# The weight sums for the seven-product down projection: from VectorE in the mix to GpSimd in the mix and VectorE in the up projection; the sample's squares split in one piece

## The chip, the cores and the metric

One NeuronCore of one Trainium2 chip runs the whole step in one launch. The metric is the time of an execution on the device, in microseconds. Engines are named as the profile names them: PE (matmul), PEld (its weight loads), DVE (VectorE), ACT (ScalarE), POOL (GpSimd), SP (SyncE, which here only issues transfers).

## The reference, cut to what matters

One layer of a decoder is computed for 512 prompt tokens and 64 sample tokens (8 sequences of 8). Two attention branches come first. What the change touches comes behind them:

```python
br_fox = o_fox @ w_br_fox;  br_nsa = o_nsa @ w_br_nsa          # 512 -> 1024 each
mix = sigmoid(mg[:, :1024]) * br_fox + sigmoid(mg[:, 1024:]) * br_nsa   # mg = h @ w_in[:, last 2048]
x = x + gt1 * (mix @ w_out)
h = rms_norm(x, norm2_g) * (1 + sc2) + sh2
u = relu(h @ w_up)                                             # 1024 -> 4096
y = x + gt2 * ((u * u) @ w_down)                               # 4096 -> 1024
```

All of it is in float32, and all weights are read from HBM once per launch.

## The kernel before, in words

**Precision.** PE multiplies in a rounded format. Every float32 operand is therefore split into a high part (a copy by ACT into the rounded format) and a low part (operand minus high part, on DVE): `split`, lines 113 and 132 in the profile. A product is made of three matmuls, high by high, low by high, high by low. A weight is loaded into a raw tile by SP, split, and only then multiplied. The raw tiles of most weights come from one ring of three, with the tag "raw".

**Seven products.** The up projection (from its fourth pair of weight columns on) and most of the down projection use Strassen's scheme in the form with seven products instead of eight. It needs sums and differences of weight quarters. For down, with rows 0 to 1535 of `w_down` as upper half, rows 1536 to 3071 as lower half, and columns halved, they are b12 - b11, then b22 minus that, b22 - b11 and b21 - b22. The kernel makes them ahead of time: `down_sums(pool, k)` (line 1956) handles one of twelve row blocks of 128. It loads two tiles of 128 x 1024 ("td", SP, line 1961), makes four differences of 128 x 512 in place (DVE, line 101, the helper `tt`), and stores both tiles to HBM tiles `tD` (POOL, line 1966). The "td" tiles come from a ring of three. The products T1 to T4 of down read `tD` back ("wdrT").

**The mix** (`mix_part`, line 1878). For each of eight column blocks e and each branch x: a gate product "mg" (48 matmuls), tanh on ACT into "mgt", a branch product "br" (24 matmuls), and on DVE (line 110) mgt = (mgt + 1) * br, which frees the PSUM banks of br. PE has four banks for these, so it can be two products ahead. Behind both branches the two mgt are added (POOL for e below 7, line 1950) and the sum is split into `mix2`. In e = 1 to 6 two calls of `down_sums` follow. Weights are raw tiles "wmr" and "wbr", split into "wmh"/"wml" and "wbh"/"wbl".

**Out and up** (`out_part`, `mlp_up`, line 2177). The output projection's weights "wo" are split into rooms that lie where the mix's tiles were; wo3 lies over the td tiles. In `mlp_up` each pair n of weight columns goes through seven products "up<n>a", "up<n>b" and "up<n>e", 12 matmuls each, in an order written out by hand. The sums of the up weights (`pair_weights`, line 2158; "sums<-pu") are POOL's from pair 5 on. DVE splits the weights ("wp") and reads PSUM between the products that accumulate into one bank ("u<-up6b" and so on). `squares_out` relus, squares and stores u to HBM: `sD` (blocks for the seven-product part) or `uD`.

**Down** (`mlp_down`, line 2241). Seven products p = 0 to 6 over three chunks c of 512 rows each; PE's groups "dn" are the prompt's, "dns" the sample's (p = 0, 1, 4, 5). For dns, `sample_part` (line 2111) loads one block of squares ("sr", POOL), and splits it into a room "sa": one load, one ACT copy, one subtraction per chunk. The first block is made ahead, in up (`u_load`, line 2119). The tile that "sr" is loaded to, with the tag "us", lies over the last u tile of up (u15) in the built program, so it waits for u15's store.

**What sets the order.** Each engine runs its instructions in the order that the tile scheduler gives them when the program is built. An instruction that waits holds everything behind it on its engine. `issue_after` and `pinned` only push an instruction behind another one in that order; they add no wait on the chip. The helper `dma` keeps the transfers of one queue in the order in which they are written. A tile from a ring waits until the tile that had its place is read for the last time, a stored one until its store has landed.

Of the kernel before, what the change touches and what calls it, by code (L numbers as in the profile page):

```python
# [6 lines left out]
F32 = mybir.dt.float32  # L7
# [7 lines left out]
P = 128  # L15
# [31 lines left out]
class Step:  # L47
# [1830 lines left out]
    def mix_part(self, pq, pr, mix2):  # L1878
# [55 lines left out]
        for e in range(NK):  # L1934
            if e == 0:
                ws = [weights(0, x) for x in range(2)]
                for k in range(8):
                    self.split(oH[:, k], oL[:, k], self.oT[:, k])
                m = [gate(e, x, ws[x][0], True) for x in range(2)]
                for x in range(2):  # L1940
                    branch(e, x, ws[x][1], m[x])
            else:
                m = []
                for x in range(2):
                    mg, br = weights(e, x)
                    m.append(gate(e, x, mg))
                    branch(e, x, br, m[x])
            if e == NK - 1:
                self.wo0 = self.out_weights(0)
            (nc.gpsimd if e < NK - 1 else nc.vector).tensor_tensor(m[0], m[0], m[1], op=OP.add)  # L1950
            self.split_pack(mix2[:, e], m[0])
            if 0 < e < NK - 1:
                for k in range(2 * e - 2, 2 * e):
                    self.down_sums(pq, k)

    def down_sums(self, pool, k):

        b = [pool.tile([P, D], F32, tag="td", bufs=3, name=f"td{k}_{i}") for i in range(2)]
        for i in range(2):
            r0 = SQ * 512 * i + P * k  # L1960
            self.nc.sync.dma_start(b[i], self.I["w_down"][0, r0:r0 + P, :])
        (b11, b12), (b21, b22) = [[t[:, 512 * h:512 * h + 512] for h in range(2)] for t in b]
        for out, x, y in ((b11, b12, b11), (b12, b22, b12), (b22, b22, b11), (b21, b22, b21)):
            self.tt(out, x, y, OP.subtract)
        for i in range(2):
            self.nc.gpsimd.dma_start(self.tD[k // 2][:, k % 2, i], b[i])
# [144 lines left out]
    def sample_part(self, pool, tag, blk, room):  # L2111

        x = pool.tile([P, 4, NS], F32, tag=tag, bufs=3, name=f"sr{blk}_{self.turn}")
        self.turn += 2
        self.dma("gpsimd", x, self.sD[blk][:, 2048:2304].rearrange("p (k t) -> p k t", k=4))
        self.split(room[:, :, 0:NS], room[:, :, NS:P], x)
        return room

    def u_load(self, q):
# [6 lines left out]
        elif q == 2:  # L2126
            self.first_sample = self.sample_part(self.praw, "raw", 0, self.both[:, 4096:4608].rearrange("p (k t) -> p k t", k=4))
# [49 lines left out]
    def mlp_up(self, pu, h3):  # L2177
# [27 lines left out]
        for n in range(FIRST, NP + 1):  # L2205
# [15 lines left out]
            if 0 <= n - NP + 6 < 4:  # L2221
                self.u_load(n - NP + 6)
# [18 lines left out]
    def mlp_down(self, pf):  # L2241
# [26 lines left out]
        left = [self.ph.tile([P, 2, 4, 256], F32, tag="h3", bufs=2, name=f"s2{i}") for i in range(2)]  # L2268
        left = [left[c // 2][:, c % 2] for c in range(SQ)]
# [26 lines left out]
        for p, key in enumerate(("11", "21", "T3", "T2", "T1", "22", "T4")):  # L2296
            pbs = [self.mmb(f"dn{p}{m}") for m in range(2)]
            sample = {0: 0, 1: 1, 4: 0, 5: 1}.get(p)
            if sample is not None and p != 5:
                sb = self.accb(f"dns{p}")  # L2300
            for c in range(SQ):
# [12 lines left out]
                if sample is not None:  # L2314
                    x = self.first_sample if p + c == 0 else self.sample_part(
                        pf, "us", c + SQ * sample, pf.tile([P, 4, P], F32R, tag="sa", bufs=3, name=f"sa{p}_{c}"))
                    for k in range(4):
                        for e in range(2):
                            self.mm(sb, x[:, k], w[e][:, k], c + k + e == 0 and p != 5, c == SQ - 1 and k + e == 4 and p != 4)
# [30 lines left out]
        for blk in range(2 * SQ, NBLK):  # L2350
# [8 lines left out]
            if not last:  # L2359
                x2 = [self.pb.tile([P, 4, D], F32, tag="x", bufs=1, name="x2b")]  # L2360
                x2 = [x2[0][:, i] for i in range(4)] + [pf.tile([P, D], F32, tag="x2s", bufs=1, name="x2s")]
                for i, (t0, m) in enumerate(TILES):
                    self.dma("sync", x2[i][:m], self.x2D[:m, i])
                with self.tc.issue_after(self.last_mm):
                    gp = self.gate_prompt(self.ph, 40, 1.0, "2", tag="h3", bufs=2)
                    gx = pf.tile([P, NT], F32, tag="u", bufs=3, name="gx2")[:, 0:512]
                    gs = self.gate_sample(self.ph, 40, 1.0, "2", gx.rearrange("p (k b t) -> p k b t", k=NK, t=8), tag="h3", bufs=2)
# [218 lines left out]
```

## Time and profile before

| what | us |
|---|---|
| median of 3 runs (1206.57 to 1213.69) | 1207.56 |
| the profiled execution's own time | 1211.11 |
| its span, first to last instruction | 1209.4 |
| PE busy | 1144.4 |
| DVE busy | 814.3 |
| ACT busy | 582.0 |
| POOL busy | 203.1 |

The stages in the profiled execution, by PE's groups: attention to about 587, the mix from there to 759, out to 817, up to 1008 (with down's first chunk pulled in at 999), down to the end. In lists of groups a row gives line, engine, operation, tiles (out<-in), shapes and count, then busy time and mean duration of one, then the idle time of the engine just before these instructions and what ended it. In timelines a row gives start and duration, then the engine; a bracket gives the idle time before it and the releaser. In tables by stretch there are, for each engine, busy time and instructions; then PE's granted clock (1.00 is full), the busy share of the transfer engines and GB/s.

### The profile page before, as it was taken

How to read it: one execution, taken by the hardware profiler on the slowest of the kernel's cores; microseconds unless marked ns; L12 is line 12 of the kernel's file. 1: busy time of each engine (PE TensorE's matmuls, PEld its weight loads, DVE VectorE, ACT ScalarE, POOL GpSimd, SP SyncE). 2: the span in 40 equal slices, each digit the busy share in tenths (PEclk: the TensorE clock that was granted, in tenths of full speed). 3: DMA queues.
4: the chain of work that ended last, by engine and by line, in shares of the span. 5: the costliest groups of instructions: out<-in, count | busy, mean ns of one | idle time of the engine just before them, and what ended most of it. 6: DMA issues, size and time to landing. Idle time of an engine off the chain costs nothing.

```text
span 1209.4 us, 24525 instructions
## 1 busy us (share of the span) xinstructions
PE 1144.4 (95%) x9051; PEld 979.7 (81%) x9051; DVE 814.3 (67%) x2000; ACT 582.0 (48%) x1183; POOL 203.1 (17%) x254
## 2 busy tenths in 40 slices
PE   4999999999999999999879899999999996999998
PEld 4887789999666656776779789889999995888887
DVE  3787785686788856665555463677877753788686
ACT  2554453454777755545412222447555654564520
POOL 3303000001211130000312120001556401101100
PEclk9999999999999899999989999999999998999999
DMA  9897556794776359989989983437454538857742
GB/s 219 212 250 229 156 152 220 249 329 160 254 236 209 99 164 311 299 284 293 308 260 270 264 262 110 130 93 223 150 161 151 187 102 252 308 183 264 234 133 79
DMA packets 188091, 255.48 MB, mean 211 GB/s; under 512 B 23065, under 2 KB 145634, under 8 KB 185794
## 3 DMA queue, kind: packets, MB, share of 16 engines
q1 hardware_dynamic: 150402, 185.61, 50.5%
q0 software_dynamic: 17456, 53.74, 13.6%
q10 hardware_dynamic: 20112, 14.55, 4.2%
q8 instruction: 71, 1.16, 0.4%
q14 instruction: 50, 0.41, 0.1%
HBM read 217.64 MB, written 57.12 MB: 227 GB/s over the span
## 4 chain that ended last, share of the span: by engine, by line
PE 72%; DMA 13%; DVE 6%; issue 4%; ACT 3%; SPq 1%; POOL 1%; ACTq 0%; DVEq 0%; POOLq 0%
PE dn L78 13%; PE z L78 6%; PE hid L78 6%; PE wo L78 4%; DMA td<-in_w_down 3%; PE up L78 3%; PE mg L78 3%; PE ss L78 2%; PE ct L84 2%; DMA tD<-td 2%; PE dns L78 2%; PE k L84 2%; PE br L78 2%; PE so L78 1%; PE ada L78 1%
## 5 line engine op out<-in xcount | busy, mean ns | idle before, releaser
L78 PE MATMUL z<-winh,h 128*128 128x264 f32 (+1 forms) x576 | 111.0, 286 | 0.3
L78 PEld LDWEIGHTS z<-winh,h 128*128 128x128 f32 x576 | 91.7, 190 | 2.1 <-DVE h L800 0.9
L78 PE MATMUL z<-winl,h 128*128 128x264 f32 (+1 forms) x320 | 88.2, 284 | 0.1
L78 PE MATMUL mg<-hH,wmh 128*128 128x288 f32 x256 | 77.0, 302 | 9.9 <-DVE mgt L110 9.5
L78 PE MATMUL mg<-hH,wml 128*128 128x288 f32 x256 | 76.4, 300 | 0.9 <-DVE wml L132 0.9
L113 ACT ACTIVATE xh<-ct 128x256 fp32r<-128x256 f32 x128 | 48.0, 384 | 56.4 <-PE ct L84 29.5
L78 PE MATMUL mg<-hL,wmh 128*128 128x288 f32 x256 | 74.1, 300 | 0.3 <-DMA hL<-hfd 0.3
L132 DVE TENSOR_TENSOR xl<-ct,xh 128x256 fp32r<-128x256 f32 x128 | 51.7, 420 | 14.5 <-ACT xh L113 12.7
L78 PEld LDWEIGHTS z<-winl,h 128*128 128x128 f32 x320 | 60.6, 190 | 0.3 <-DVE winl L132 0.3
L78 PEld LDWEIGHTS mg<-hH,wmh 128*128 128x128 f32 x256 | 49.4, 193 | 10.6 <-DVE mgt L110 9.8
L78 PEld LDWEIGHTS mg<-hH,wml 128*128 128x128 f32 x256 | 49.3, 193 | 1.1 <-DVE wml L132 1.1
L78 PEld LDWEIGHTS mg<-hL,wmh 128*128 128x128 f32 x256 | 48.2, 192 | 0.8 <-DMA hL<-hfd 0.7
L101 DVE TENSOR_TENSOR td<-td,td 128x512 f32<-128x512 f32 x24 | 16.6, 690 | 47.0 <-DMA td<-in_w_down 46.8
L78 PE MATMUL br<-oH,wbh 128*128 128x288 f32 x128 | 38.7, 302 | 8.1 <-DVE mgt L110 8.1
L78 PE MATMUL hid<-xh,w1hlk 128*128 128x512 f32 (+1 forms) x160 | 45.2, 370 | 1.2 <-ACT xh L113 1.2
L132 DVE TENSOR_TENSOR wp<-sums,wp 128x1024 fp32r<-128x1024 f32 x26 | 39.3, 1520 | 8.8 <-ACT wp L113 8.3
L78 PE MATMUL hid<-xh,w1hlv 128*128 128x512 f32 (+1 forms) x160 | 44.0, 362 | 0.4 <-ACT xh L113 0.4
L132 DVE TENSOR_TENSOR wp<-pu,wp 128x512 fp32r<-128x512 f32 (+1 forms) x26 | 31.2, 1206 | 16.5 <-ACT wp L113 16.0
L84 PE MATMUL ct<-identF,ro 128*128 128x128 f32 x256 | 36.4, 282 | 6.1 <-DVE ro L116 5.1
L113 ACT ACTIVATE wbh<-wbr 128x512 fp32r<-128x512 f32 x16 | 10.0, 631 | 61.0 <-DMA wbr<-in_w_br_nsa 38.1
L113 ACT ACTIVATE u<-u 128x1152 f32<-128x1152 f32 x29 | 33.7, 1161 | 10.2 <-DVE u L101 9.7
L78 PE MATMUL br<-oL,wbh 128*128 128x288 f32 x128 | 38.0, 297 | 0.0
(1180 smaller groups left out, 3670.8 us busy)
## 6 DMA issues: line engine op xcount, KB each, us to landing
adw<-in_w_ada SPq DMA_DIRECT2D x16, 1024.0 KB
foxD<-in_cache_fox_kv SPq DMA_DIRECT2D x128, 128.0 KB
fr<-foxD SPq DMA_DIRECT2D x28, 512.0 KB
sr<-in_cache_nsa_kv SPq DMA_DIRECT2D x112, 128.0 KB
cpg<-in_cache_nsa_kv SPq DMA_DIRECT2D x104, 128.0 KB
pu<-in_w_up SPq DMA_DIRECT2D x26, 512.0 KB
wdr<-in_w_down SPq DMA_DIRECT2D x26, 512.0 KB
td<-in_w_down SPq DMA_DIRECT2D x24, 512.0 KB
```

What stands on the lines that cost most here:

```text
L78: ins = self.nc.tensor.matmul(out, a, b, start=start, stop=stop, skip_group_check=True)
L84: ins = self.nc.tensor.transpose(out, in_, self.identF[:n, :n])
L101: self.nc.vector.tensor_tensor(out, a, b, op=op)
L113: return self.nc.scalar.activation(out, in_, f, **kw)
L132: self.splits.append((eng or self.nc.vector).tensor_tensor(l, x, h.bitcast(F32), op=OP.subtract).ins)
```

## The change

- In the mix, `down_sums` runs for eight of the twelve row blocks, in e = 1 to 6 (one block or two each). The loads, the four differences and the stores are all POOL's now, in its own queue. The two mgt are added by DVE in all e.
- The other four row blocks are made in up, two at a time: loaded by SP in n = 5 and 8 (two transfers of 1 MB each), the four differences (now 128 x 2 x 512) on DVE in n = 6 and 9, stored by POOL in n = 7 and 10. Their tile is the room "x" of the pool `pb`, which held R before and holds the first split token blocks ("as") behind.
- `u_load` comes one n later.
- In down, `sample_part` makes all blocks of one product in one piece: for p = 0 blocks 1 and 2 (128 x 8 x 64), for p = 1, 4, 5 three blocks (128 x 12 x 64). Loads stay one per block. The room "sa" is in the pool `ph` ("h3"); the raw tile "us" is a single one, and in the built program it lies over T0, an operand of up that PE reads for the last time in pair 15's first product E. The three tiles of differences "s2" and the late gates move to a tag "late" of the pool `pf`.

```diff
-            (nc.gpsimd if e < NK - 1 else nc.vector).tensor_tensor(m[0], m[0], m[1], op=OP.add)
+            nc.vector.tensor_tensor(m[0], m[0], m[1], op=OP.add)
             self.split_pack(mix2[:, e], m[0])
-            if 0 < e < NK - 1:
-                for k in range(2 * e - 2, 2 * e):
-                    self.down_sums(pq, k)
+            for k in ((), (0,), (1,), (2, 3), (4,), (5, 6), (7,), ())[e]:
+                b = [pq.tile([P, 1, D], F32, tag="td", bufs=3, name=f"td{k}_{i}") for i in range(2)]
+                with self.tc.issue_after(self.last_mm):
+                    self.down_rows(b, k, "gpsimd")
+                    self.down_sums(b, nc.gpsimd)
+                    self.down_store(b, k)
...
+    def down_rows(self, b, k, eng):
+        n = b[0].shape[1]
+        for i in range(2):
+            r0 = SQ * 512 * i + P * k
+            self.dma(eng, b[i], self.I["w_down"][0, r0:r0 + n * P, :].rearrange("(k p) c -> p k c", p=P))
+    def down_sums(self, b, eng):
+        (b11, b12), (b21, b22) = [[t[:, :, 512 * h:512 * h + 512] for h in range(2)] for t in b]
         for out, x, y in ((b11, b12, b11), (b12, b22, b12), (b22, b22, b11), (b21, b22, b21)):
-            self.tt(out, x, y, OP.subtract)
+            eng.tensor_tensor(out, x, y, op=OP.subtract)
+    def down_store(self, b, k):
+        n = b[0].shape[1]
         for i in range(2):
-            self.nc.gpsimd.dma_start(self.tD[k // 2][:, k % 2, i], b[i])
+            self.dma("gpsimd", self.tD[k // 2][:, k % 2:k % 2 + n, i], b[i])
...
-    def sample_part(self, pool, tag, blk, room):
+    def sample_part(self, pool, tag, blks, room):
-        x = pool.tile([P, 4, NS], F32, tag=tag, bufs=3, name=f"sr{blk}_{self.turn}")
+        x = pool.tile([P, 4 * len(blks), NS], F32, tag=tag, bufs=3 if tag == "raw" else 1, name=f"sr{blks[0]}_{self.turn}")
         self.turn += 2
-        self.dma("gpsimd", x, self.sD[blk][:, 2048:2304].rearrange("p (k t) -> p k t", k=4))
+        for i, blk in enumerate(blks):
+            self.dma("gpsimd", x[:, 4 * i:4 * i + 4], self.sD[blk][:, 2048:2304].rearrange("p (k t) -> p k t", k=4))
         self.split(room[:, :, 0:NS], room[:, :, NS:P], x)
...
-            if 0 <= n - NP + 6 < 4:
-                self.u_load(n - NP + 6)
+            if n in (5, 8):
+                kd = 8 if n == 5 else 10
+                td = self.pb.tile([P, 2, 2, D], F32, tag="x", bufs=1, name=f"td{kd}")
+                td = [td[:, i] for i in range(2)]
+                self.down_rows(td, kd, "sync")
+            if n in (6, 9):
+                with self.pinned((self.splits[-1],)):
+                    self.down_sums(td, self.nc.vector)
+            if n in (7, 10):
+                self.down_store(td, kd)
+            if 0 <= n - NP + 5 < 3:
+                self.u_load(n - NP + 5)
...
-        left = [self.ph.tile([P, 2, 4, 256], F32, tag="h3", bufs=2, name=f"s2{i}") for i in range(2)]
-        left = [left[c // 2][:, c % 2] for c in range(SQ)]
+        left = [pf.tile([P, 4, 256], F32, tag="late", bufs=3, name=f"s2{c}") for c in range(SQ)]
...
+            if sample is not None:
+                blks = tuple(range(SQ * sample + (p == 0), SQ * sample + SQ))
+                xs = self.sample_part(pf, "us", blks, self.ph.tile([P, 4 * len(blks), P], F32R, tag="h3", bufs=2, name=f"sa{p}"))
+                xs = xs if p else self.first_sample + xs
```

Three places show how the built order moves. The first is DVE at the start of the mix, behind the splits of the attention outputs ("oL"). Before, six of these eleven rows are differences of td, among the weight splits and the rows that free br's banks:

```order
L132 TENSOR_TENSOR oL<-oT,oH 128x576 x4
L101 TENSOR_TENSOR td_1_9629<-td_1_9629,td_0_9628 128x512
L101 TENSOR_TENSOR td_0_9638<-td_0_9638 128x512
L101 TENSOR_TENSOR td_1_9629<-td_1_9629 128x512
L101 TENSOR_TENSOR td_0_9638<-td_1_9639,td_0_9638 128x512
L132 TENSOR_TENSOR wml_1_9437<-wmr_1_0_9438,wmh_1_9436 128x1024
L101 TENSOR_TENSOR td_1_9639<-td_1_9639,td_0_9638 128x512
L110 SCALAR_TENSOR_TENSOR mgt_9304<-mgt_9304,br_9376 128x288
L132 TENSOR_TENSOR wml_1_9531<-wmr_1_0_9532,wmh_1_9530 128x1024
L101 TENSOR_TENSOR td_0_9840<-td_0_9840 128x512
L110 SCALAR_TENSOR_TENSOR mgt_9304<-mgt_9304,br_9377 128x288
```

With the change the same stretch of DVE's order is:

```order
L132 TENSOR_TENSOR oL<-oT,oH 128x576 x8
L132 TENSOR_TENSOR wml_1_9437<-wmr_1_0_9438,wmh_1_9436 128x1024
L110 SCALAR_TENSOR_TENSOR mgt_9304<-mgt_9304,br_9376 128x288
L132 TENSOR_TENSOR wml_1_9531<-wmr_1_0_9532,wmh_1_9530 128x1024
L110 SCALAR_TENSOR_TENSOR mgt_9304<-mgt_9304,br_9377 128x288
L132 TENSOR_TENSOR wbl_1_9443<-wbr_1_0_9444,wbh_1_9442 128x512
```

No td row stands ahead of a weight split or of a row that frees a bank any more, through the whole mix. The second place is DVE in up, around the PSUM reads of pair 6. Before:

```order
L132 TENSOR_TENSOR wp_3_12279<-sums,wp_3_12279 128x1024
L132 TENSOR_TENSOR wp_2_12398<-sums,wp_2_12398 128x1024
L101 TENSOR_TENSOR u_12295<-up6b,sums 128x288
L101 TENSOR_TENSOR u_12295<-up6e,u_12295 128x288
L132 TENSOR_TENSOR wp_0_12516<-pu_0_12408,wp_0_12516 128x512
L101 TENSOR_TENSOR u_12415<-up7b,sums 128x288
```

With the change (td_12193 holds row blocks 8 and 9):

```order
L132 TENSOR_TENSOR wp_3_12242<-sums,wp_3_12242 128x1024
L1970 TENSOR_TENSOR td_12193<-td_12193 128x2x512
L132 TENSOR_TENSOR wp_2_12365<-sums,wp_2_12365 128x1024
L1970 TENSOR_TENSOR td_12193<-td_12193 128x2x512
L101 TENSOR_TENSOR u_12258<-up6b,sums 128x288
L1970 TENSOR_TENSOR td_12193<-td_12193 128x2x512
L101 TENSOR_TENSOR u_12258<-up6e,u_12258 128x288
L132 TENSOR_TENSOR wp_0_12485<-pu_0_12375,wp_0_12485 128x512
L1970 TENSOR_TENSOR td_12193<-td_12193 128x2x512
L101 TENSOR_TENSOR u_12382<-up7b,sums 128x288
```

Two of the four differences now stand ahead of the read of up6b, and three ahead of that of up6e; pair 9 has the same pattern. The third place is ACT at the start of down, where the weights of the next product (wd_1), the last store of u and the sample's copies (sa) stand in one row. With the change:

```order
L113 ACTIVATE wd_1h<-wdr_1_0_13673 128x1024
L163 DMA uD_11461<-u_13338 128x1152
L113 ACTIVATE wd_1h<-wdr_1_1_13677 128x1024
L113 ACTIVATE sa_13474<-sr_157_13475 128x8x64
L113 ACTIVATE as_13574<-a_02_13575 128x1024
L113 ACTIVATE wd_2h<-wdr_2_0_13721 128x1024
L113 ACTIVATE wd_2h<-wdr_2_1_13725 128x1024
L113 ACTIVATE sa_13617<-sr_159_13618 128x12x64
```

The sa row stands behind both wd_1 rows, as the first sa row of before did; the second sa row is now the whole of product 1. On PE, the dns of chunks 1 and 2 of product 0 now follow each other, 16 matmuls, ahead of the dn of chunk 2.

More of the change, by code (lines that the diff above doesn't have):

```diff
@@ L2109, in token_room @@
         return t[:, 0], t[:, 1]
-    def sample_part(self, pool, tag, blk, room):
-        x = pool.tile([P, 4, NS], F32, tag=tag, bufs=3, name=f"sr{blk}_{self.turn}")
+    def sample_part(self, pool, tag, blks, room):
+        x = pool.tile([P, 4 * len(blks), NS], F32, tag=tag, bufs=3 if tag == "raw" else 1, name=f"sr{blks[0]}_{self.turn}")
         self.turn += 2
-        self.dma("gpsimd", x, self.sD[blk][:, 2048:2304].rearrange("p (k t) -> p k t", k=4))
+        for i, blk in enumerate(blks):
+            self.dma("gpsimd", x[:, 4 * i:4 * i + 4], self.sD[blk][:, 2048:2304].rearrange("p (k t) -> p k t", k=4))
         self.split(room[:, :, 0:NS], room[:, :, NS:P], x)
-        return room
+        return [room[:, 4 * i:4 * i + 4] for i in range(len(blks))]
     def u_load(self, q):
@@ L2126, in u_load @@
         elif q == 2:
-            self.first_sample = self.sample_part(self.praw, "raw", 0, self.both[:, 4096:4608].rearrange("p (k t) -> p k t", k=4))
+            self.first_sample = self.sample_part(self.praw, "raw", (0,), self.both[:, 4096:4608].rearrange("p (k t) -> p k t", k=4))
     def split_u(self, u2, u):
@@ L2314, in mlp_down @@
                 if sample is not None:
-                    x = self.first_sample if p + c == 0 else self.sample_part(
-                        pf, "us", c + SQ * sample, pf.tile([P, 4, P], F32R, tag="sa", bufs=3, name=f"sa{p}_{c}"))
                     for k in range(4):
                         for e in range(2):
-                            self.mm(sb, x[:, k], w[e][:, k], c + k + e == 0 and p != 5, c == SQ - 1 and k + e == 4 and p != 4)
+                            self.mm(sb, xs[c][:, k], w[e][:, k], c + k + e == 0 and p != 5, c == SQ - 1 and k + e == 4 and p != 4)
             for m, pb in enumerate(pbs):
@@ L2360, in mlp_down @@
                 x2 = [self.pb.tile([P, 4, D], F32, tag="x", bufs=1, name="x2b")]
-                x2 = [x2[0][:, i] for i in range(4)] + [pf.tile([P, D], F32, tag="x2s", bufs=1, name="x2s")]
+                x2 = [x2[0][:, i] for i in range(4)] + [pf.tile([P, D], F32, tag="late", bufs=3, name="x2s")]
                 for i, (t0, m) in enumerate(TILES):
@@ L2364, in mlp_down @@
                 with self.tc.issue_after(self.last_mm):
-                    gp = self.gate_prompt(self.ph, 40, 1.0, "2", tag="h3", bufs=2)
+                    gp = self.gate_prompt(pf, 40, 1.0, "2", tag="late", bufs=3)
                     gx = pf.tile([P, NT], F32, tag="u", bufs=3, name="gx2")[:, 0:512]
-                    gs = self.gate_sample(self.ph, 40, 1.0, "2", gx.rearrange("p (k b t) -> p k b t", k=NK, t=8), tag="h3", bufs=2)
+                    gs = self.gate_sample(pf, 40, 1.0, "2", gx.rearrange("p (k b t) -> p k b t", k=NK, t=8), tag="late", bufs=3)
             todo = [(i, 512 * hf, 512) for i in ((4, 0, 1, 2, 3) if last else range(5)) for hf in range(2)]
```

4 lines of the change are left out of this document (removed).

## Prediction

> **What bounds the kernel now.** I read the chain of work that ended last, then PE's waits by stage, then the table by stretch, then the timelines around each wait.
>
> ```profile
> PE 72%; DMA 13%; DVE 6%; issue 4%; ACT 3%; SPq 1%; POOL 1%; ACTq 0%; DVEq 0%; POOLq 0%
> PEclk9999999999999899999989999999999998999999
> ```
>
> PE carries the chain; the 13% of DMA is where to look. From the mix on, PE waits in two places (waits of PE: releaser, total, times, longest):
>
> ```profile
> PE mg L78 <- DVE mgt L110: 9.5, 1, 9.5
> PE br L78 <- DVE mgt L110: 8.1, 6, 2.2
> PE dns L78 <- DVE sa L132: 10.2, 1, 10.2
> ```
>
> The first two are the mix, 17.6 us; the third is the start of down. In up PE waits nowhere for long. The stretches (PE, PEld, DVE, ACT, POOL busy, PE's clock, DMA share, GB/s):
>
> ```profile
> 602.00:612.00 10.00, 0.48 (x4) 0.25 (x2) 2.96 (x5) 0.00 (x0) 0.53 (x1) 0.65 0.85 275
> 612.00:615.00 3.00, 3.00 (x13) 3.00 (x14) 3.00 (x5) 0.14 (x1) 0.17 (x1) 0.50 0.73 187
> 630.00:640.00 10.00, 10.00 (x78) 10.00 (x77) 5.24 (x8) 1.53 (x2) 2.49 (x3) 1.00 0.92 283
> 696.00:701.00 5.00, 5.00 (x26) 5.00 (x27) 2.44 (x4) 0.49 (x1) 0.94 (x2) 0.66 1.02 306
> 1018.00:1025.00 7.00, 0.00 (x0) 0.00 (x0) 0.29 (x1) 0.42 (x1) 3.87 (x8) 0.50 0.95 299
> 1025.00:1031.00 6.00, 5.49 (x13) 4.33 (x14) 3.00 (x4) 3.46 (x5) 2.51 (x5) 0.50 0.99 354
> ```
>
> Each long wait is paid twice: while PE stands the clock falls to 0.50, and PE runs at half rate for 3 to 6 us behind it. The row at 630 shows that PE runs full while the transfers are as busy as ever: bandwidth is not what stops the mix. What does is the order on DVE:
>
> ```profile
> 598.79 8.60 SPq L1961 DMA_DIRECT2D td<-in_w_down  x2
> 609.04 0.69 DVE L101 TENSOR_TENSOR td<-td,td 128x512 f32<-128x512 f32 x1 [11.83 <-DMA td<-in_w_down]
> 611.38 0.45 DVE L110 SCALAR_TENSOR_TENSOR mgt<-mgt,br 128x288 f32<-128x288 f32 x1
> 611.89 0.61 PE L78 MATMUL mg<-hH,wmh 128*128 128x288 f32 x1 [9.52 <-DVE mgt L110]
> ...
> L101 DVE TENSOR_TENSOR td<-td,td 128x512 f32<-128x512 f32 x24 | 16.6, 690 | 47.0 <-DMA td<-in_w_down 46.8
> ```
>
> SP's td load waits for the place of a tile still being stored, DVE stands 11.83 us in a td row, the mgt row behind it frees a bank late, and PE waits for that bank. In the whole mix such rows held DVE 47.0 us.
>
> **The mix.** No td row is on DVE there any more, so this wait has no carrier. What PE does without it shows at the end of the stage, where the td work is over (chain, a gate and the last branch product):
>
> ```profile
> 721.19 6.38 PE mg L78 x48
> ...
> 756.15 3.19 PE br L78 x24
> ```
>
> From 721.19 to 759.34 stand four pairs, 9.54 us each. The branch products of e = 0 end at 611.89 - 9.52 = 602.37, and fourteen pairs follow: 14 x 9.54 = 133.5 us against 759.34 - 602.37 = 157.0. At most 23.5 us go: the waits and the slow clock behind them. I take 22.5, for small waits that may come instead. The other end is 12: half of it, if the weights of the first pairs turn out as late as the td rows. DVE also gets seven more sums of the two mgt, each twice the size of the mgt row above (about 2 x 0.45 = 0.9 us), and loses 48 differences of 0.69, so it is less busy than before.
>
> POOL now has the whole chain of eight blocks. Its rows:
>
> ```profile
> L2165 POOL TENSOR_TENSOR sums<-pu,pu x11: 1275/1330/2931, 852.0 to 965.9; 128x512 f32<-128x512 f32 x11
> tD<-td POOLq DMA_DIRECT2D x24, 512.0 KB, 4.7
> x<-in_x_prompt POOLq DMA_DIRECT2D x4, 512.0 KB, 5.9
> L1966 POOL DMA_DIRECT2D tD<-td x24 | 13.0, 541 | 102.6 <-DVE td L101 100.8 <-issue 1.7
> 766.05 1.05 ACT L113 ACTIVATE wo3h<-wor 128x1024 fp32r<-128x1024 f32 x1
> 769.33 0.62 PE L78 MATMUL wo<-wo3h,mix 128*128 128x512 f32 x2
> ```
>
> One block: the second load waits for the store of the block before, some 2.2 us after the first load's issue; it lands 5.9 later, about 8.1 in all. Three differences of 1.33 to 1.6, a store's issue of 0.54, the fourth difference, another 0.54: some 14 us. Eight are 112 us; from about 587, the start of the mix, to about 700. The first instruction that needs the rooms of td again is ACT's split of wo3, 6.7 us behind the end of the mix, so at about 743 now. 43 us of cover: POOL's slower arithmetic costs nothing. If that cover were gone, wo3 would wait for POOL's last store.
>
> **The up projection.** Eight differences of 1024 elements come to DVE. A row of that size and the reads of PSUM that stand behind it:
>
> ```profile
> L132 DVE TENSOR_TENSOR wp<-sums,wp x26: 1209/1226/2320, 848.3 to 984.5; 128x1024 fp32r<-128x1024 f32 x26
> 895.04 1.23 DVE L132 TENSOR_TENSOR wp<-sums,wp 128x1024 fp32r<-128x1024 f32 x1
> 897.22 1.51 DVE L132 TENSOR_TENSOR wp<-sums,wp 128x1024 fp32r<-128x1024 f32 x1 [0.95 <-ACT wp L113]
> 899.16 0.46 DVE L101 TENSOR_TENSOR u<-up6e,u 128x288 f32<-128x288 f32 x1
> 901.84 1.60 PE up6b L78 x12
> 903.43 1.60 PE up6e L78 x12
> ```
>
> PE's product at 901.84 adds into the bank that u<-up6b reads, the one at 903.43 into that of u<-up6e. With 1.23 per difference the first fits into DVE's 0.95 us of waiting for ACT but for 0.3, the second pushes u<-up6b to about 900.5 and its end to 901.0, 0.8 us ahead of PE; the third pushes u<-up6e's end to some 902.7, 0.7 ahead. So nothing by the plain duration. At 2.32 each, the same rows end at about 904 and 906, and PE stands some 2.5 us, twice in the stage with a little behind it: 6 us. I take 1.5, nearer to nothing, since DVE idles about a quarter of each pair and POOL is free part of the time. The Trainium skill (SBUF — State Buffer, on the shared port pair) states that a VectorE instruction with two SBUF inputs and a GpSimd one that reads SBUF exclude each other for a whole instruction; the spread from 1209 to 2320 ns agrees. By that rule alone all eight would take the long form, and this term would be 6 and the sum 4.5 us smaller.
>
> The loads and stores (8 MB in all) move to up from the mix; SP's td rows stand ahead of the up weights of pair 8 and 11, which then land some 5 us later, with a pair's time (11.2 us, seven products of 1.60) between their split and their use. I cost them at nothing; it would be up to 5 us per block without that slack.
>
> **Down.** What holds PE at 1015 is the place of "us": its load waits for u15's store.
>
> ```profile
> 1015.98 1.06 ACT L113 ACTIVATE wd_1h<-wdr 128x1024 fp32r<-128x1024 f32 x1 [0.20 <-DMA wdr<-in_w_down]
> 1015.81 2.48 DVE L132 TENSOR_TENSOR wd_1l<-wdr,wd_1h 128x1024 fp32r<-128x1024 f32 x2 [1.74 <-ACT wd_1h L113]
> 1021.13 0.57 POOL L163 DMA_DIRECT2D sr<-sD  x1 [50.88 <-DMA wdr<-in_w_down]
> 1025.03 0.43 DVE L132 TENSOR_TENSOR sa<-sr,sa 128x256 fp32r<-128x256 f32 x1 [6.74 <-ACT sa L113]
> 1025.51 0.79 PE L78 MATMUL dns<-wd_1h,sa 128*128 128x512 f32 x1 [10.24 <-DVE sa L132]
> ...
> 1025.51 3.78 PE dns L78 x8
> 1029.29 6.62 PE dn L78 x24
> 1035.91 1.81 PE dns L78 x8
> 1037.73 5.44 PE dn L78 x24
> ...
> 696.00 0.40 PE L78 MATMUL br<-oH,wbh 128*128 128x288 f32 x1 [2.16 <-DVE mgt L110]
> ```
>
> The stop costs 10.24, and at half clock (3.78 - 1.81) + (6.62 - 5.44) = 3.2 more: 13.4. With the change "us" lies over T0, last read three products before up ends, so the loads land about 1001. But ACT takes the copy only behind wd_1h, at 1017.0; with 0.6 us for it, and DVE behind its two wd_1l rows (to 1018.3) plus 0.7, sa is there at about 1019.0. PE waits from 1025.51 - 10.24 = 1015.27, some 3.7 us instead of 10.24. Whether the clock falls in 3.7 us is open: a wait of 2.16 at 696 went with the 0.66 above. I count 2 of the 3.2 as lost. Next late is product 1: its load of three blocks waits for the single "us", so DVE's sa at 1019.0, then three issues (0.57 each), 5 to 6 to land (POOL's loads of x: 5.9), the split: about 1028, when PE gets there; I count 1. Left: 13.4 - 3.7 - 2 - 1 = 6.7; I take 6.5. The ends are 13.4 and nothing. The Trainium skill (TensorE: Matmul & The Clock Gate, Part 1) puts the fall at about 3.4 us of idleness in a window that runs free. By it the clock may stay up and this term would be 8.5.
>
> **Sum.** 1211.1 - 22.5 + 1.5 - 6.5 = 1183.6 for the profiled execution. The median of the runs shown is 3.5 below it: 1180.1. The runs spread over 7 us, so I say 1181.
>
> **Rivals.** *The wait passes to the weights* (1191, chance 0.14): POOL's loads meet those of wmr and wbr, and half of the mix's gain stays: 12 instead of 22.5. For it: DMA 1.02 near 700. Against it: full PE at 630 under the same traffic.
>
> *Down's wait stays* (1187, 0.14): the second sa, in one piece, comes later than three single ones, and 6.5 becomes nothing. For it: ACT's order, and one buffer. Against it: the load starts 20 us earlier.
>
> *Up stands behind the td rows* (1186 to 1190, 0.08): 6 to 9 us instead of 1.5. For it: the 2320 ns. Against it: DVE's idle time there.
>
> *POOL outlasts the mix* (1220, 0.04), the slower side. If a block took over 18.7 us, its last store (587.5 + 8 blocks + 4.7) would land behind 743 and wo3 would hold ACT, and PE from about 746, as its read of wo3h stands 3.3 us behind the split before. From some 22.5 us per block the whole gain is gone; at 24.1 the store lands at 785, the wait is 39, and the time 1220. For it: 2931 ns differences. Against it: four of these, the longest of eleven, make a block of only 20 us.
>
> *It doesn't do what it says*: the td rows are gone from DVE's order in the mix, so this is only possible if something else were equally late, the first rival.
>
> **How the numbers follow.** The forecast has 0.60, with a range of its own from 1174 to 1187. Below it stand full terms everywhere, 23.5 and 13.4: 1171. Above it the rivals on the faster side reach 1191, with both of the smaller ones together 1197. So 1171 to 1197. A measurement of this kernel tells about 1% from no change, 12 us: faster means under 1195.5. All but the slow rival and parts of the first two, if they come together, lie there: 0.89 faster, 0.07 within, 0.04 slower.
>
> **What would show it.** Right: in the mix no wait of PE for mgt over 1 us, DVE waiting for no td load, 9.5 us per pair from 602 on, POOL's last td store before 725; in up, waits of PE for u of under 2 us; in down, a wait of dns of 3 to 5 us. Wrong: waits of mg or br for wml or wbl; the split of wo3 waiting for POOL; a wait for sa of 10 us; td rows in up that wait for their load.

## The result, and the profile after

| | before | after |
|---|---|---|
| median, us (4 runs each) | 1207.07 (1205.09 to 1213.69) | 1192.69 (1192.07 to 1193.66) |
| ratio, 95% interval | | 0.9872 [0.9834, 0.9911] |
| span of the profiled execution, us | 1209.4 | 1190.4 |

The change is faster by 14.4 us. The prediction was 1181, with 1171 to 1197: the time lies inside the range, in the right direction, but the likeliest case's own range ended at 1187, and its gain was 26. A second measurement of the same kernel gave 0.9867 [0.9847, 0.9888].

Where the 19.0 us between the two profiled spans come from is read best stage by stage. The marks are taken from PE's timeline: the end of the branch products of e = 0, the end of the last branch product, the first product of up, up's first seven-product pair (up3a), the first dns, the first long run of dn, the last dn.

| stage, us | before | after | difference | predicted |
|---|---|---|---|---|
| up to the end of the first branch products | 602.4 | 601.2 | -1.2 | |
| mix, fourteen pairs | 157.0 | 133.4 | -23.5 | -22.5 |
| out | 57.6 | 57.5 | 0 | 0 |
| up, first part | 39.3 | 39.3 | 0 | 0 |
| up, seven-product pairs (with a part of down) | 151.6 | 164.0 | **+12.4** | **+1.5** |
| start of down | 51.5 | 45.2 | -6.3 | -6.5 |
| rest of down | 146.0 | 146.0 | 0 | 0 |

Two of the three terms came out within a microsecond. The third one, up, is eight times its size, and it is nearly the whole difference between 26 and 14. (The medians differ by less than the two profiles, since the profiled execution of before was 1211.11, some 4 us above its median, and that of after, 1192.07, is not. Which stage of before is shorter in its other runs isn't known, as there is one profile of it.)

PE's waits in the profile after (releaser, total, times, longest):

```profile
PE dns L78 <- DVE sa L132: 4.0, 1, 4.0
PE up8b L78 <- DVE u L101: 3.6, 1, 3.6
...
PE up9b L78 <- DVE u L101: 2.6, 1, 2.6
...
PE up5b L78 <- DVE u L101: 1.3, 1, 1.3
```

The mix's two rows are gone, and the wait of dns is 4.0 instead of 10.2. In their place stand three waits of over 1 us in up that before did not have.

**The mix.** The chain of work, the waits of DVE from 586 to 760, and a row of the table by stretch:

```profile
601.23 6.35 PE mg L78 x48
607.57 3.19 PE br L78 x24
...
731.48 3.19 PE br L78 x24
```

```profile
DVE wml L132 <- ACT wmh L113: 51.2, 13, 6.3
DVE mgt L110 <- PE br L78: 14.1, 11, 7.4
```

```profile
601.00:611.00 10.00, 10.00 (x78) 10.00 (x77) 3.80 (x7) 1.80 (x4) 1.97 (x4) 1.00 1.10 312
```

PE runs from 601 to 734.7 without a stop; DVE waits for no transfer. The stretch from 601 to 611, in which PE stood for 9.5 us before, is now full at clock 1.00, although the DMA share stands at 1.10: traffic as such does not stop the mix. POOL's chain and the next use of its rooms:

```profile
587.07 1.11 POOL L163 DMA_DIRECT2D td<-in_w_down  x2
...
704.76 0.58 POOL L163 DMA_DIRECT2D tD<-td  x1 [0.30 <-POOL td L1970]
```

```profile
741.38 1.05 ACT L113 ACTIVATE wo3h<-wor 128x1024 fp32r<-128x1024 f32 x1
```

Eight blocks in 118 us are 14.7 per block (14 was predicted), and 36 us are left between POOL's last issue and the split of wo3.

**Up.** DVE's and POOL's timelines (the bracket is the idle time before, and the releaser), then SP's one wait for a store of td and where SP and ACT issue at that time:

```profile
861.26 0.46 DVE L101 TENSOR_TENSOR u<-up5b,sums 128x288 f32<-128x288 f32 x1 [1.59 <-DMA sD<-u]
...
899.99 0.46 DVE L101 TENSOR_TENSOR u<-up8b,sums 128x288 f32<-128x288 f32 x1 [3.83 <-DMA sD<-u]
...
913.52 2.32 DVE L1970 TENSOR_TENSOR td<-td 128x1024 f32<-128x1024 f32 x1
915.76 2.31 DVE L132 TENSOR_TENSOR wp<-sums,wp 128x1024 fp32r<-128x1024 f32 x1
917.99 2.28 DVE L1970 TENSOR_TENSOR td<-td 128x1024 f32<-128x1024 f32 x1
920.19 0.44 DVE L101 TENSOR_TENSOR u<-up9b,sums 128x288 f32<-128x288 f32 x1
```

```profile
883.40 0.69 POOL L163 DMA_DIRECT2D tD<-td  x1 [1.99 <-DVE td L1970]
...
914.72 2.27 POOL L2176 TENSOR_TENSOR sums<-pu 128x512 f32<-128x512 f32 x1
916.95 2.24 POOL L2176 TENSOR_TENSOR sums<-pu,sums 128x512 f32<-128x512 f32 x1
```

```profile
SPq L163 <- DMA tD<-td: 6.2, 1, 6.2
```

```profile
888.72 0.92 SPq L163 DMA_DIRECT2D td<-in_w_down  x2
```

```profile
888.63 1.50 ACTq L163 DMA_DIRECT2D sD<-u  x3
```

```profile
895.00:901.00 6.00, 2.43 (x17) 2.19 (x16) 2.17 (x3) 3.54 (x4) 0.21 (x1) 0.94 1.07 379
...
921.00:924.00 3.00, 3.00 (x14) 3.00 (x14) 3.00 (x5) 0.03 (x1) 0.25 (x1) 0.50 0.74 289
```

There are two kinds of stop. Before up5b and up8b DVE waits for a **store of u**: u has two tiles, so u8 is written where u6 was, and u6's stores, issued by ACT at 888.63, are still on their way at 899.97, more than 11 us later. SP issued the two td loads, 2 MB, in the same moment. Before up9b it is **DVE's row of work**: two td rows and a weight split, 2.3 us each, stand ahead of the read of up9b, while POOL adds. Behind the stops of 3.6 and 2.6 us the clock falls again (0.50 in the last row). PE waits for no split of the up weights.

**Down.** The chain, with ACT's row ahead of it:

```profile
1004.70 0.61 ACT L113 ACTIVATE sa<-sr 128x512 fp32r<-128x512 f32 x1
```

```profile
1006.15 0.70 DVE sa L132
...
1006.89 6.70 PE dns L78 x16
1013.59 5.45 PE dn L78 x24
1019.04 1.59 PE dns L78 x7
```

The sa row comes behind both wd_1 rows of ACT, as the order showed, and PE stands 4.0 us (3.7 were predicted). The sixteen dns take 6.70 instead of 2 x 1.81, so 3.1 us go to the slow clock (2 were counted as lost). Product 1 follows without a wait (1 was counted).

### The profile page after: what moved, and what is told of

Same layout as the page of the kernel before. It is cut to its first block, busy times and chain, and to the rows that moved or that the text cites. A ratio compares the mean times of both kernels' runs of the same rounds, so it can differ in the third digit from the quotient of the medians.

```text
span 1190.4 us, 24438 instructions
## 1 busy us (share of the span) xinstructions
PE 1142.7 (96%) x9051; PEld 979.5 (82%) x9051; DVE 807.7 (68%) x1960; ACT 582.4 (49%) x1176; POOL 249.8 (21%) x291
## 4 chain that ended last, share of the span: by engine, by line
PE 77%; DVE 7%; DMA 7%; ACT 4%; issue 2%; SPq 1%; POOL 1%; ACTq 0%; DVEq 0%; POOLq 0%
PE dn L78 13%; PE mg L78 9%; PE hid L78 7%; PE z L78 6%; PE br L78 4%; PE wo L78 4%; PE up L78 3%; PE ss L78 2%; PE ct L84 2%; PE dns L78 2%; PE so L78 2%; PE k L84 2%; DMA sD<-u 2%; PE ada L78 2%; PE sp L84 1%
## 5 line engine op out<-in xcount | busy, mean ns | idle before, releaser
L132 DVE TENSOR_TENSOR wml<-wmr,wmh 128x1024 fp32r<-128x1024 f32 x14 | 19.9, 1419 | 51.2 <-ACT wmh L113 51.2
L113 ACT ACTIVATE mgt<-mg 128x288 f32<-128x288 f32 x32 | 12.8, 409 | 57.2 <-PE mg L78 57.2
L132 DVE TENSOR_TENSOR wp<-pu,wp 128x512 fp32r<-128x512 f32 (+1 forms) x26 | 30.6, 1181 | 14.8 <-ACT wp L113 14.8
L113 ACT ACTIVATE u<-u 128x1152 f32<-128x1152 f32 x29 | 33.6, 1159 | 10.4 <-DVE u L101 10.1
L78 PE MATMUL br<-oH,wbl 128*128 128x288 f32 x128 | 37.7, 295 | 0.0
(1181 smaller groups left out, 3709.0 us busy)
```

The source lines that it names most:

```text
L78: ins = self.nc.tensor.matmul(out, a, b, start=start, stop=stop, skip_group_check=True)
L113: return self.nc.scalar.activation(out, in_, f, **kw)
L132: self.splits.append((eng or self.nc.vector).tensor_tensor(l, x, h.bitcast(F32), op=OP.subtract).ins)
```

## Experiments

All times of a group were taken on one chip, with the kernel before beside them (its medians: 1211.25 in the first group, 1210.02 in the second, 1208.77 in the third), so ratios are compared. Where an expectation gives a time, it stands beside 1207. One table for all, with the stages of the one profile of each kernel; down runs from the first dns to the last dn.

| kernel | ratio, 95% interval | mix | up's pairs | down |
|---|---|---|---|---|
| before | 1 | 157.0 | 151.6 | 197.5 |
| the change | 0.9872 [0.9834, 0.9911] | 133.4 | 164.0 | 191.1 |
| after_again | 0.9867 [0.9847, 0.9888] | 134.9 | 165.8 | 191.2 |
| up_none | 0.9742 [0.9719, 0.9765] | 133.4 | 151.7 | 189.9 |
| up_traffic | 0.9775 [0.9740, 0.9810] | 133.4 | 157.8 | 190.6 |
| up_pool | 0.9808 [0.9782, 0.9834] | 133.4 | 159.9 | 191.7 |
| ten | 0.9774 [0.9751, 0.9797] | 133.4 | 155.0 | 191.6 |
| up_actq | 0.9778 [0.9755, 0.9802] | 133.4 | 153.6 | 190.9 |
| twelve | 0.9790 [0.9758, 0.9822] | 133.4 | 153.1 | 190.8 |
| mix_sum_pool | 0.9916 [0.9892, 0.9939] | 138.9 | 167.0 | 190.6 |
| mix_sp | 0.9938 [0.9915, 0.9961] | 141.3 | 166.6 | 190.0 |
| down_old | 0.9923 [0.9898, 0.9947] | 135.1 | 165.1 | 196.6 |
| sa_first | 0.9924 [0.9905, 0.9943] | 133.4 | 166.5 | 195.4 |
| best | 0.9809 [0.9787, 0.9831] | 134.2 | 153.2 | 196.8 |

Within up, each pair's up<n>a comes twice on PE. From the second up<n>a of one pair to that of the next it takes 11.2 us where nothing stops PE. What stands above that, by the pair whose second up<n>a ends the stretch (n = 6 holds the wait before up5b, 7 the td rows of the first group, 9 the wait before up8b, 10 the td rows of the second):

| kernel | n = 6 | 7 | 9 | 10 |
|---|---|---|---|---|
| the change | 1.6 | 1.3 | 5.2 | 4.3 |
| after_again | 3.9 | 1.3 | 6.3 | 2.5 |
| up_none | 0 | 0 | 0 | 0 |
| up_traffic | 6.0 | 0 | 0 | 0 |
| up_pool | 4.1 | 0 | 1.0 | 0 |
| ten | 2.0 | 1.3 | 0 | 0 |
| up_actq | 0 | 1.3 | 0 | 1.3 |

### What costs in up: all, the traffic, the rows

up_none takes the whole block out (and lets down read `tD[(...) % 4]`); up_traffic takes out only the differences, so both compute down with wrong weights; up_pool gives them to POOL. The two edits shown are those of up_traffic and up_pool.

```diff
-            if n in (6, 9):
-                with self.pinned((self.splits[-1],)):
-                    self.down_sums(td, self.nc.vector)
```

```diff
-                    self.down_sums(td, self.nc.vector)
+                    self.down_sums(td, self.nc.gpsimd)
```

> Leaves out the last four row blocks of down's weight sums altogether (no loads, differences, stores in up; down reads the first eight blocks' tiles in their place), so it computes part of the product from wrong weights. Every theory that puts the change's loss in up down to these rows expects up to run as it did before the change, 12.2 us less than in the profile of the change: about 1180.5 us against 1192.7, and no wait of PE for u over 1 us. If up stays at some 203 us, the loss comes from something else that was moved.

> Keeps the loads and stores of the four row blocks in up and leaves out their eight differences on DVE (the stored weights are wrong, so down's result is). Theory: two causes side by side, the td loads that delay the stores of u (waits before up5b and up8b, 6.7 us with the slow clock) and the td rows in DVE's order (waits before up6b, up6e, up9b, 5.5 us): 1187 us. Rival 1, the rows on DVE alone: about 1181. Rival 2, the traffic alone: about 1192.

> The eight differences in up are made by POOL instead of DVE; all else as in the change. Theory of two causes: the waits before up6b and up9b go, those before up5b and up8b stay: 1187 us, if POOL's own sums for the next pair are not made late (rival: they are, PE then waits for wp, up to 1192). Traffic alone: 1192. Rows on DVE alone: 1181.

up_none's up takes 151.7 us, as long as before: all 12.4 us come from the four row blocks. Its ratio is 0.013 below that of the change, some 16 us; of the 3 or 4 us that aren't in up, 1.2 are in down, and the rest is not placed.

up_traffic loses 6.1 us in up, all of it at one place:

```profile
PE up5b L78 <- DVE u L101: 4.2, 1, 4.2
```

So the traffic alone is enough for a stop, which rival 1 excludes, although the time, 0.9775, is the one it gave. But not at n = 8, where the changed kernel has its longest stop. The reason stands in where SP's second td load is issued, 7 us ahead of the stores of u at 888.52, not with them:

```profile
847.05 0.89 SPq L163 DMA_DIRECT2D td<-in_w_down  x2
...
881.54 0.96 SPq L163 DMA_DIRECT2D td<-in_w_down  x2
```

```profile
850.10 1.43 ACTq L163 DMA_DIRECT2D sD<-u  x3
```

The first load, 3 us ahead of the stores, stops PE in both kernels. The second does so where it falls on the stores. In the changed kernel it is late because it waits 6.2 us for the place of the first two blocks, whose last store POOL issued at 883.40, behind the last td row of DVE; in up_traffic SP waits for no store of td. So the causes are not side by side, as the theory had it: the rows make the second load late, and the late load makes the store of u late.

up_pool bears this out from the other side: with no td row on DVE nothing is lost at 7 and 10, 4.1 at 6 and only 1.0 at 9, where SP's second load is issued at 882.88, 5.8 us ahead of the stores. In turn 1.0 is lost at n = 11 and 2.7 at n = 13, where the change loses nothing and 0.6; POOL's own sums ahead of them come later, which may be why.

### The changed kernel again

> The changed kernel as it is, a second profile and its times on the chip of the other runs of this group. Expected 0.987 of the kernel before, as at first. If the waits before up5b and up8b differ by microseconds from those of the first profile, at the same code, they hang on how transfers meet and not on the order of an engine alone.

The same code lost 3.9 us at n = 6 and 6.3 at 9, where it had lost 1.6 and 5.2. With up_traffic's 6.0 and ten's 2.0, code that in up is the same as far as that place loses between 1.6 and 6.0 there. The rows of DVE at n = 7 cost 1.3 in each run that has them. So the stops before up5b and up8b hang on how transfers meet. The second group of rows (n = 10) cost 4.3 and 2.5 with the same code, and 1.3 in up_actq below, so that stop doesn't hang on DVE's order alone either.

### The same loads behind the stores

```diff
-                self.down_rows(td, kd, "sync")
+                self.down_rows(td, kd, "scalar")
```

> The four td loads in up are issued by ACT, in the queue of the stores of u and behind them, instead of by SP; differences on DVE and stores by POOL as in the change. Theory (the td loads delay the stores of u that DVE's next u row waits for): the waits before up5b and up8b shrink to under 1 us, those before up6b and up9b stay: 5 to 7 us less than the change, 0.982 of before. Rival (the td rows on DVE make the stores of u late, or the td bytes slow everything wherever they are issued): no difference, 0.987, waits before up5b and up8b as before.

This run puts the stores first. ACT's timeline shows the loads in the same queue as the stores, and behind them, and DVE's shows what is left of the wait:

```profile
887.92 1.43 ACTq L163 DMA_DIRECT2D sD<-u  x3
...
897.46 1.44 ACTq L163 DMA_DIRECT2D sD<-u  x3
899.00 1.03 ACTq L163 DMA_DIRECT2D td<-in_w_down  x2
```

```profile
892.20 0.46 DVE L101 TENSOR_TENSOR u<-up8b,sums 128x288 f32<-128x288 f32 x1 [0.27 <-DMA sD<-u]
...
901.12 0.46 DVE L101 TENSOR_TENSOR u<-up9b,sums 128x288 f32<-128x288 f32 x1 [2.31 <-PE up9b L78]
```

The stores that ACT issued at 887.92 had landed at 892.2, after 4.3 us, where the same stores took 11.3 in the change. The next stores, with the td loads 1.5 us behind them in the queue, had landed by 901.12, at most 3.7 us after their issue: DVE's row there writes u9, where u7 was, and waited for PE last. The bytes, the rows and the stores of td are the same, and 10.4 us are gone, from the medians of one group (1193.01 to 1182.58) as well as from up (164.0 to 153.6; 165.8 in the second profile of the change). What is left are 1.3 us for each group of rows. The expected gain, 5 to 7, was too small: with the loads out of the way the rows of the second group cost 1.3 as well, not 4.3. Moving the load also moved the first reads of up5b and of up8b ahead of splits in DVE's order, so at n = 6 the two edits aren't told apart; at n = 9 the row waited for the store and for nothing else, in the change as here, so its place in the order can't have made the store land early. The load also came some 10 us later (899.00 instead of 888.72). The run shows that the store lands early when no td load is issued ahead of it or with it; it doesn't separate the place in the queue from the time of issue.

### Other places for the blocks

ten makes ten blocks in the mix; twelve all of them, in a room for two blocks at a time, each loaded ahead of the differences of the one before, and takes the block out of up. Of each edit the main lines are shown.

```diff
-            for k in ((), (0,), (1,), (2, 3), (4,), (5, 6), (7,), ())[e]:
+            for k in ((), (0,), (1,), (2, 3), (4, 5), (6, 7), (8, 9), ())[e]:
...
-            if n in (5, 8):
-                kd = 8 if n == 5 else 10
+            if n == 5:
+                kd = 10
...
```

```diff
-            for k in ((), (0,), (1,), (2, 3), (4,), (5, 6), (7,), ())[e]:
...
+            if e == 0:
+                self.tdr = self.keep.tile([P, 4, 1, D], F32, tag="r1", bufs=1, name="tdr")
+            for k in ((0, 1), (2, 3), (4, 5), (6, 7), (8, 9), (10, 11), (12,), ())[e]:
+                with self.tc.issue_after(self.last_mm):
+                    if k < 12:
+                        self.down_rows([self.tdr[:, 2 * (k % 2) + i] for i in range(2)], k, "gpsimd")
+                    if k:
+                        b = [self.tdr[:, 2 * ((k - 1) % 2) + i] for i in range(2)]
+                        self.down_sums(b, nc.gpsimd)
+                        self.down_store(b, k - 1)
...
```

> POOL makes ten row blocks in the mix instead of eight, and up only the last two (load at n = 5, differences at n = 6, store at n = 7). POOL's pace in the profile of the change is 14.7 us per block, so its tenth store lands at about 739, some 4 us ahead of wo3's split. Theory: the waits around n = 8 and 9 go (9.5 us), those around 5 and 6 stay (2.6): 1183 us. Rival: POOL outlasts the mix, wo3 waits, and some 5 us of it come back: 1188 or more.

> POOL makes all twelve row blocks in the mix, with room for two blocks at a time (in the place of x2, which is free between the attention outputs and out), the loads of a block issued ahead of the differences of the one before; nothing of it in up. Theory: a block takes POOL some 10 to 11 us instead of 14.7, since it no longer waits 4 to 5 us for each load; the last store lands before 735, the mix keeps its 133.4 us, up takes the 151.7 us it took without td work, and the whole about 12 us less than the change: 0.976 of before. Rival: POOL outlasts the mix, x2 comes late, and out waits for it: out longer than 57.5 us and 0.980 or more.

Both did in their stages what was expected. ten: the second group's stops are gone, the first group's stay, out is 58.3 instead of 57.5, and the ratio 0.9774 is lower than that of the change by 11 to 12 us (9.5 expected). twelve: POOL needs 10.6 us per block, 600.07 to 727.8 for twelve:

```profile
600.07 2.10 POOL L163 DMA_DIRECT2D tdr<-in_w_down  x4 [7.34 <-DVE oL L132]
...
727.22 0.57 POOL L163 DMA_DIRECT2D tD<-tdr  x1 [0.30 <-POOL tdr L1974]
```

The mix is 133.4, out 58.0, up 153.1. Still its ratio is not lower than ten's. In its profile the first branch products end at 607.4, where mix_sp's has 604.6 and the twelve others 599.0 to 602.4; it is the slowest of its four runs (1181.12 to 1187.69). Whether twelve makes that part slower or it was chance isn't settled.

### What made the mix stop

The change does three things there at once: the differences leave DVE, the loads leave SP, the sums of the two mgt leave POOL. Two kernels undo the second and the third.

```diff
-                    self.down_rows(b, k, "gpsimd")
+                    self.down_rows(b, k, "sync")
```

```diff
-            nc.vector.tensor_tensor(m[0], m[0], m[1], op=OP.add)
+            (nc.gpsimd if e < NK - 1 else nc.vector).tensor_tensor(m[0], m[0], m[1], op=OP.add)
```

> The change, but the td loads of the eight blocks of the mix are issued by SP again, among the loads of the mix's weights, where they wait for the store of the block before; the differences stay POOL's. Theory (the stops of the mix came from DVE's order alone): the mix stays within 2 us of 133.4 us, 0.987 to 0.989 of before. Rival (a td load that waits at the head of SP's queue makes the weights of the mix late): waits of PE for wml or wbl, and the mix goes back to between 140 and 157 us, 0.993 to 1.007.

> The change, but the two mgt are added by POOL again (e below 7), behind its td work. Theory (an engine that waits for a td load must not carry a row that frees a buffer PE depends on): POOL's sum stands behind differences that wait 4 to 5 us for their loads, up to 14.7 us per block; mgt has two buffers, so ACT's next tanh waits, the banks of mg stay full, and PE waits in the mix again: some 5 to 20 us more than the change, 0.991 to 1.004 of before. Rival (only the loads' place in SP's queue mattered, or the rows on DVE): no difference, 0.987.

My theory for mix_sp fell: the mix lost 7.9 us (133.4 to 141.3), where at most 2 were expected. The waits of SP's queue, of ACT and of PE in its mix show how:

```profile
SPq L163 <- DMA tD<-td: 47.5, 10, 8.2
```

```profile
ACT wbh L113 <- DMA wbr<-in_w_br_nsa: 27.8, 3, 14.4
ACT wbh L113 <- DMA wbr<-in_w_br_fox: 24.8, 3, 10.9
```

```profile
PE mg L78 <- ACT mgt L113: 5.4, 4, 3.9
```

A td load at the head of SP's queue waits for POOL's store, the loads of wbr wait behind it, ACT waits for them in the row of wbh, and the tanh that frees PE's bank waits behind wbh. The rival had the size, 140 to 157, but PE waits for the tanh and for no split of wml or wbl.

mix_sum_pool lost 5.5 us in the mix (138.9), in the range given, by the path given:

```profile
ACT mix L113 <- POOL mgt L1950: 36.0, 5, 10.3
```

```profile
PE mg L78 <- ACT mgt L113: 3.4, 2, 2.5
```

POOL's sum stands behind its td work, ACT waits up to 10.3 us for it in a row of mix, and the tanh behind that is late. So of the 23.5 us SP's queue alone, put back, takes 7.9 and POOL's sum alone 5.5; if the parts add up, some 10 are left for DVE's rows. No run puts DVE's rows back alone, so their part isn't shown. Without either of the other two moves a part of the gain is lost.

### The start of down

down_old puts the sample's part back as it was (the loop with one block, the rooms too); sa_first keeps the change and puts product 1's weight splits behind the sample's.

```diff
...
+                    x = self.first_sample if p + c == 0 else self.sample_part(
+                        pf, "us", (c + SQ * sample,), pf.tile([P, 4, P], F32R, tag="sa", bufs=3, name=f"sa{p}_{c}"))
```

```diff
+                if p == 0:
+                    sa_last = (self.splits[-1], self.last_high)
...
-                w = chunk(key, c)
+                w = chunk(key, c, sa_last if p == 1 else None)
```

> The change with the sample's part of down as it was before (one load, one copy, one subtraction per block, rooms as before, so that the load waits for the last store of u again). Theory: down's start goes back from 45.2 us (end of up to the first long stretch of dn) to the 51.5 us of before, 6.3 us, 0.992 of before; the rest is as in the change. Rival (the start is set by the weights of down, not by this load): no difference, 0.987.

> The change, with the weight splits of down's second product put behind the sample's split of the first in the orders of ACT and DVE. Theory: what is left of down's wait, 4.0 us and some 3.1 us of slow clock behind it, is only this order; sa is there at about 1000 instead of 1006.8, PE does not stop, and down's start takes 38 us instead of 45.2: 0.981 of before. Rival (the second product's weights, split later, are late in turn): PE waits for wd_0l or wd_1l, and 3 us or less are gained, 0.984 to 0.987.

down_old: the wait is back, and the ratio is 0.005 to 0.006 higher than that of the change, 6 us:

```profile
PE dns L78 <- DVE sa L132: 9.8, 1, 9.8
```

sa_first: the theory fell. PE no longer stops at product 0, but it does at product 1, 4.9 us instead of 4.0. The chain:

```profile
1006.47 9.35 DMA wdr<-in_w_down
...
1017.45 0.74 ACT sa L113
1018.21 0.97 DVE sa L132
1019.23 6.85 PE dns L78 x21
```

The splits of product 1's weights, put behind sa, free their raw tiles later, so the next weights are loaded later, ACT waits for them until 1015.9, and product 1's sa row stands behind that split. This stop takes back what the first one gave: from the first dns to the first one of product 4 it is 83.1 us, and 83.2 in the change. The 4.3 us by which down is longer than in the change all lie behind that, at a wait that the change doesn't have:

```profile
PE gs L84 <- ACT gp L113: 2.5, 1, 2.5
```

```profile
1144.39 0.78 ACT L113 ACTIVATE u<-ud 128x512 fp32r<-128x512 f32 x2 [4.07 <-DMA ud<-uD]
```

"gp" and "gs" are the late gates. ACT's gp row stands behind its split of a block of squares (ud<-uD), and that block's load, issued by POOL at 1137.50, lands 6.9 us later; in the change it was issued at 1132.73 and landed in 4.8. The clock is 0.50 behind this stop (1146 to 1149). What makes that load late isn't shown: POOL issued it 1.8 us after SP's first load of x2, in the change 0.6 us ahead of that one. SP's loads of down's last weights are late as well: they begin 3.2 us ahead of the last dns (1114.13), in the change 8.5 (1106.48).

### The edits together

ten's list, up_actq's queue and sa_first's order.

> Three edits of earlier runs together: ten row blocks by POOL in the mix, the last two in up with their loads in ACT's queue behind the stores of u, and the sample's split ahead of the weight splits in down. Theory: up takes 151.6 us and one stretch of 1.3 us for the rows on DVE, down's start some 38 us, mix and out as in the change: 11 us from up and 7 from down, 0.972 of before, about 1176 us beside 1210. Without the gain in down: 0.978.

Up took 153.2 us, as expected; down 196.8, near sa_first's 195.4, with the same wait before gs (3.0 us). So 0.9809 is above ten and up_actq alone. The fastest versions measured that compute the whole layer are ten, 0.9774, and up_actq, 0.9778, both clear of the change's 0.9867 and not told apart, from each other or from twelve (0.9790). The two of them without sa_first's order were not tried.

## Why the prediction was right in two terms and wrong in the third

- **The mix, right.** The pace read at the end of the stage, 9.54 us per pair, held for all fourteen: 133.4 measured, 133.5 worked out. POOL's block took 14.7, not 14 (the terms of that sum add up to 14.5 or more); its cover was never near gone. What the argument left out is that the stop had two more carriers: SP's queue, worth 7.9 us when put back alone, and POOL's sums, worth 5.5. The change moved all three, so the number held. That is in part luck: the wait was put down to "the order on DVE" alone.
- **Down, right.** -6.3 against -6.5; a wait of 4.0 against 3.7. Two small errors cancel: more clock lost (3.1 instead of 2), no wait in product 1. By the rule quoted from the Trainium skill (TensorE: Matmul & The Clock Gate, Part 1), some 3.4 us of idleness in a window that runs free, the clock may or may not have stayed up behind the stop; the sixteen dns, 6.70 us instead of 3.62, show that it fell.
- **Up, wrong.** The step that failed is the sentence on the loads and stores of td, "I cost them at nothing", with the weights of pairs 8 and 11 as what would be late. It measured about 10 us (up_actq). It looked at who is queued behind the loads on SP, and those had slack (PE waited for no split of the up weights). It did not ask which other transfers are in flight at that moment and who waits for them: ACT's stores of u, with two tiles of u and DVE's next row waiting for a store. In before that wait was there already, small:

```profile
DVE u L101 <- DMA sD<-u: 1.7, 2, 1.3
```

That row of DVE's waits in up is from the profile before. Its two waits stand at pairs 12 and 13 (958.88 and 970.39), not where the loads were put; so it doesn't prove that the stores had no slack at pairs 5 and 8, but it names the row that waits for a store, and it asked for a term.

- **The rows on DVE in up**, predicted as 1.5 within 0 to 6, cost 2.6 by themselves, 1.3 per group. In the changed kernel the second group cost up to 4.3, with rows of 2.3 us one behind the other while POOL added. The mean of the eight rows was 1.71 us, between the 1.23 and the 2.32 of the sum: four took 1.21 or 1.22 and four 1.93 to 2.32, so not all eight took the long form. (With all eight in it the term would be 6 and the time 4.5 us longer; the prediction has "smaller".)
- **The rivals.** The one on up had the stage and a time, 1186 to 1190, near the measured one, but by DVE's rows, which alone cost 2.6. The weights of the mix were not late, down's wait did not stay, and POOL did not outlast the mix. So the range, which these rivals had widened to 1197, held the time for a reason that isn't among them; that is luck.

## What to carry to other kernels

A transfer that is moved is costed twice: by what stands behind it in its queue, and by the transfers of other queues that are in flight where it lands, above all stores whose tile is needed again. A wait for a store in the profile before, even one of a microsecond at another place, names the engine and the ring of tiles to look at; here, putting the new load behind that store in the store's own queue gave back 10.4 us without moving a byte less. And where a change moves one chain of work off several in-order queues, each of them may carry part of the gain, so undo them one at a time before giving the gain to one.

## What the runs showed of the hardware

- Stores of 64 to 256 KB that ACT issued took over 11 us to land where 2 MB of loads from SP's queue were issued in the same moment (888.63 to 899.97), and 4.3 us where no such load was issued ahead of them or with them (887.92 to 892.2). With the loads issued 1.5 us behind them in ACT's queue, stores had landed after 3.7 us at the latest (897.46 to 901.12). The Trainium skill (DMA: Bandwidth & Descriptors, Issuing engines are not separate DMA queues) states that transfers of all engines run on the same sixteen DMA engines and interleave, whoever starts them. The long store agrees with it. The run with the loads behind the stores adds that it matters which of two transfers is issued first.
- The length of a stop alone didn't settle whether the clock fell. It fell behind stops of PE of 2.56 us (0.50 from 921 to 924) and 3.96 us, not behind the 1.34 us before up5b, whose product took 1.85 us beside the usual 1.76, and not behind one of 2.50 us in up_pool, which ended at 952.26:

```profile
952.00:955.00 3.00, 2.74 (x20) 2.74 (x21) 1.98 (x4) 1.78 (x3) 2.84 (x3) 1.00 0.64 197
```

The wait of 2.16 us at 696 in before, which the prediction sets beside a clock of 0.66, had another of 1.73 us 4 us ahead of it (692.00).
- Profiled executions differ by some 3 us where they run the same code: the first branch products end between 599.0 and 602.1 in the change and ten kernels whose edits against it all lie behind them. A few microseconds between two single profiles say nothing; the length of a stage does.
